# First weights in quarters on SyncE's queue, x1 to x3 on ScalarE's, and the first splits in a written order

## The chip, the cores and the metric

One core of a Trainium2 chip runs the whole program. The metric is device microseconds (us) of one launch. TensorE multiplies, ScalarE and VectorE prepare its operands, GpSimd does a few small jobs, and SyncE and ScalarE issue the DMA transfers that bring inputs from the chip's memory into the on-chip memory.

## The reference, cut to what matters

The reference is a two-layer decoder trunk on 256 tokens of width 1024. Each layer is: half of a gated feed-forward block, a mixing part, and another half block. Only the very first block matters here:

```
h = h + 0.5 * swiglu(rms_norm(h, g), w_gate, w_up, w_down)      # DM = 1024, DFF = 2816
rms_norm(x, g) = x * rsqrt(mean(x*x) + 1e-6) * g
swiglu(x, wg, wu, wd) = (silu(x @ wg) * (x @ wu)) @ wd
```

Everything else (convolution, two kinds of attention, shared keys and values, the other three half blocks) is the same before and after.

## The kernel before, in words

**Layout.** The input is held transposed: `x` is 128 partitions by 8 tiles ("x0" to "x7") by 256 tokens, so tile k holds features 128k to 128k+127. All weights lie in one array of chunks, each 128 partitions by 2048 columns (1 MB), in the order of use; a chunk is used in two halves of 1024 columns, a half is eight 128x128 weight tiles.

**Precision.** Every product is made of two-part operands. A weight tile is split into a high part `wh` (ScalarE copy to a shorter format, function `hi`, L215) and a low part `wl` (VectorE subtraction of `wh` from the raw weight, `lo`, L219). The activations are split the same way: `scaled_split` (L289) writes `y` high, x times the gain (ScalarE L295, or VectorE L293 for even tiles here), and then `y` low (VectorE L296). For one weight tile, one product of 512 columns takes `wh` with both parts of `y` side by side, and one of 256 columns takes `wl` with the high part.

**The opening.** The normalisation factor is applied after the products, so the products can start before all of x is there. The first two gate tiles and the first two up tiles are summed at once, with the features k in the outer loop: for each k four `wh` products and four `wl` products (L386 to L396, output tiles `ag` and `au`). Chunk 0 and chunk 1 are packed for that: 512 columns, a "quarter" of a chunk, hold the four weight tiles of one k. Chunk 0 serves k = 0 to 3, chunk 1 serves k = 4 to 7. From chunk 2 on (the third gate tile, j = 2) a half is one output tile over all eight k.

**Queues before.** ScalarE issues the gains `vt` (L142). SyncE issues, in this order, x0, quarter 0 of chunk 0, x1, quarter 1, x2 and x3 together, the second half of chunk 0 in one transfer, x4 to x7 (L147 and L149), and then chunk 1 and chunk 2 in halves (L197 and L198), later chunks whole (L200).

**Engine orders.** A planner that simulates the program sets each engine's order of instructions, except where the code writes an order: `A`, `V`, `G` and `mmul` chain an engine's instructions when its letter is in `state["order"]`. Before, only TensorE ("P") is chained in the opening. The eight splits of x stand ahead of the block (L721 and L722), the eight squares for the mean (L403) and their sum (L407) behind it; where these land between the weight splits on ScalarE and VectorE is the planner's choice.

**Products that nobody reads.** Ten products on a constant tile run at the start (L137, output `pw`), while no data is there. Eight more (`KEEP`, L392 and L393) stand between the `wh` and `wl` products of k = 1.

**After the opening.** The sum of squares `aacc` feeds a tiny product (`anrp`), whose result is broadcast (`anbp`) and used from j = 3 on.

Of the kernel before, what the change touches and what calls it, by code (L numbers as in the profile page):

```python
# [9 lines left out]
F32 = mybir.dt.float32  # L10
# [7 lines left out]
P = 128  # L18
DM = 1024
KD = DM // P  # L20
SEQ = 256
# [16 lines left out]
CH = 2048  # L38
HC = 1024
NB = 2 * MW  # L40
WARM = 10
KEEP = {(1, 0): 8}
MASKED = 1e30

MEM_AT = 9
# [70 lines left out]
def tile_kernel(ctx: ExitStack, tc: tile.TileContext, w, xT, memT, pos, vec, hg, const, wave, bias, taps, out):  # L116
# [22 lines left out]
    nc.vector.memset(onec, 1.0 / DM)  # L139

    warm = cp.tile([P, 1], F32, name="warm")
    nc.scalar.dma_start(vt[:, :V_LG], vec[:, :V_LG])  # L142
    raw0 = wp.tile([P, CH], F32, name="raw0", tag="raw", bufs=3)
    q = HC // 2
    for tiles, cols in ((slice(0, 1), slice(0, q)), (slice(1, 2), slice(q, HC)), (slice(2, 4), slice(HC, CH)),
                        (slice(4, KD), None)):
        nc.sync.dma_start(x[:, tiles], xT[:, tiles])  # L147
        if cols is not None:
            nc.sync.dma_start(raw0[:, cols], w[0][:, cols])  # L149
    nc.scalar.activation(warm, onec, AF.Silu)  # L150
    mhalf = cp.tile([P, 16], F32, name="mhalf")
    nc.vector.memset(mhalf, -0.5)
# [188 lines left out]
    def ffn(name, y, acc, nexts, store=False, hook=None, after=None, hook_down=None, r=None, plan=None):  # L341


        state["low_at"] = LOW_AT
        plan = plan or {}
        rows_at = [j for (j, _, _), what in plan.items() if what == "rows"]
        n = KF * 2 * SEQ
        hs = cp.tile([P, n + P], F32R, name=name + "hs", tag="hs")
        hs = hs[:, GATED_AT:GATED_AT + n].rearrange("p (k h s) -> p k h s", k=KF, h=2)
        first = acc is None  # L350
        rb = None if r is None else bcast_rows(name + "nb", r)
        halves = {}
        norm = {"r": r}

        def mean():
            norm["r"] = rstd_cols(name + "nr", acc)

        def rows():
            norm["rb"] = bcast_rows(name + "nb", norm["r"])

        def planned(j, which):
            return {k: {"mean": mean, "rows": rows}.get(what, what) for (jj, w_, k), what in plan.items()
                    if (jj, w_) == (j, which)}

        def gated(j, g, h, rb):
            nc.vector.tensor_tensor(g, g, rb, op=ALU.mult)
            s = tp.tile([P, SEQ], F32, name=f"{name}s{j}", tag="s")
            state["func"] = nc.scalar.activation(s, g, AF.Silu)
            if store:
                nc.gpsimd.tensor_tensor(s, s, rb, op=ALU.mult)  # L370
            if callable(h):
                h = h()
            nc.vector.tensor_tensor(h, h, s, op=ALU.mult)
            nc.scalar.activation(hs[:, j, 0], h, AF.Copy)
            nc.vector.tensor_tensor(hs[:, j, 1], h, hs[:, j, 0].bitcast(F32), op=ALU.subtract)

        for j in range(KF):
            if hook and j > 1:
                with tc.issue_after(state["act"].ins), tc.issue_after(state["dve"].ins), \
                        tc.issue_after(state["sync"].ins):  # L380
                    hook(j)
            if first and j == 0:

                four = [psum(f"{name}{'gu'[i % 2]}{i // 2}") for i in range(4)]
                it = tiles_of(4)
                state["order"] = "P"  # L386
                for k in range(KD):
                    wts = [next(it) for _ in four]
                    for o, (wh, _) in zip(four, wts):
                        mmul(o, wh, y[:, k].rearrange("p a s -> p (a s)"), start=k == 0, stop=False)  # L390
                    for at in range(2):
                        for i in range(KEEP.get((k, at), 0)):  # L392
                            mmul(pw, busy[:, :P], busy, start=True, stop=True)  # L393
                        if at == 0:
                            for o, (_, wl) in zip(four, wts):
                                mmul(o[:, :SEQ], wl, y[:, k, 0], start=False, stop=k == KD - 1)  # L396
                state["order"] = ""
                acc = new_acc(name + "acc0")
                behind(nc.scalar.dma_start(cst, const), state["act"])

                sq = cp.tile([P, KD, SEQ], F32, name="sq0", tag="kv")
                for k in range(KD):
                    nc.scalar.activation(sq[:, k], x[:, k], AF.Square)  # L403
                n = KD
                while n > 1:
                    n //= 2
                    add = nc.vector.tensor_tensor(acc if n == 1 else sq[:, :n].rearrange("p k s -> p (k s)"),  # L407
                                                  sq[:, :n].rearrange("p k s -> p (k s)"),
                                                  sq[:, n:2 * n].rearrange("p k s -> p (k s)"), op=ALU.add)
                    if n == KD // 2:  # L410
                        behind(add, state["dve"])
            if first and j < 2:
                pg, pu = four[2 * j:2 * j + 2]
            else:

                at = ("sc", 2) if first and j == 2 else ()
                pg, pu = psum(f"{name}g{j}", *at), psum(f"{name}u{j}", *at)
                if j == 0:

                    wts = [list(tiles_of(1)) for _ in range(2)]  # L420
                    for ks in (range(KD - 1), (KD - 1,)):
                        for o, wt in zip((pg, pu), wts):
                            for k in ks:
                                mm2(o, wt[k], y, k, k == 0, k == KD - 1)
                else:
                    mm_group2(pg, y, planned(j, "g"))
                    mm_group2(pu, y, planned(j, "u"))
            if j == 0 and "mean" not in plan.values() and r is None:
                mean()
            if rb is None and j < rows_at[0]:  # L430
                halves[j] = pg, pu
                if j < 2:
                    halves[j] = both_halves(f"{name}gs{j}", pg, "g"), both_halves(f"{name}h{j}", pu, "h")
                continue
            if rb is None:
                rb = norm["rb"]
            halves[j] = pg, pu
            for i in sorted(halves):
                g, h = halves.pop(i)
                if i > 1 or not rows_at:  # L440
                    g, h = both_halves(f"{name}gs{i}", g, "g"), (lambda i=i, h=h: both_halves(f"{name}h{i}", h, "h"))
                gated(i, g, h, rb)
        if after:
            tables(after)
        ys = [y_tiles(f"{name}y{i}", Y_AT.get(f"{name}y{i}", 16)) for i in range(len(nexts))]
        acc = new_acc(name + "acc")
        it = tiles_of(KD * KF // 8)
        for m in range(KD):
            po = psum(f"{name}o{m}")
            if hook_down:  # L450
                with tc.issue_after(state["act"].ins):
                    hook_down(m)

            both_sums = m < KD - 1
            for k in range(KF):
                if both_sums:
                    mm2(po, next(it), hs, k, k == 0, k == KF - 1)
                else:
                    mm3(po[:, :SEQ], next(it), hs, k, k == 0, k == KF - 1)
            if store:  # L460
                d = both_halves(f"{name}d{m}", po, "g") if both_sums else po[:, :SEQ]
                nc.vector.scalar_tensor_tensor(x[:, m], d, 0.5, x[:, m], op0=ALU.mult, op1=ALU.add)
                nc.sync.dma_start(out[m], x[:, m])
                continue
            if both_sums:
                d = both_halves(f"{name}d{m}", po, "g")
                nc.vector.scalar_tensor_tensor(d, d, 0.5, rb, op0=ALU.mult, op1=ALU.mult)
            else:
                d = tp.tile([P, SEQ], F32, name=f"{name}d{m}", tag="g")
                nc.vector.scalar_tensor_tensor(d, po[:, :SEQ], 0.5, rb, op0=ALU.mult, op1=ALU.mult)  # L470
            nc.vector.tensor_tensor(x[:, m], d, x[:, m], op=ALU.add)
            for yy, g in zip(ys, nexts):
                state["ends"] = scaled_split(yy, x[:, m], m, g)
            square_sum(f"{name}q{m}", acc, x[:, m], m == 0)
        state["low_at"] = 0
        return ys, acc
# [241 lines left out]


    y = y_tiles("y0")  # L720
    for k in range(KD):  # L721
        scaled_split(y, x[:, k], k, V_FFN1, k % 2 == 0)  # L722
    kv0 = []

    def prepare(j):
# [797 lines left out]
```

## Time and profile before

| | |
|---|---|
| median of 3 runs | 945.51 us (945.45 to 945.63) |
| profiled execution, its own time | 946.09 us |
| its span on the core | 944.3 us |
| TensorE busy | 937.6 us, 99% of the span |
| VectorE busy | 716.4 us, 76% |
| ScalarE busy | 563.2 us, 60% |
| granted TensorE clock in the page's slices | 9 tenths or more in all 40 |

The span runs from the first to the last instruction of the program in one profiled execution; what that execution's own time has beyond it (946.09 - 944.3 = 1.8 us) lies outside the program's instructions. Rows of the timeline give the start, the duration, the engine, the source line, the tiles written and read, and in square brackets how long the engine had been idle and what ended the idle time. SPq and ACTq are SyncE's and ScalarE's sequencers issuing DMA transfers.

### The profile page before, as it was taken

To read this page: it belongs to the slowest core of one execution; us is meant where nothing else is said; L and a number is where in the kernel's file an instruction comes from. 1 tells how busy PE (TensorE), PEld (TensorE's weight loads), DVE (VectorE), ACT (ScalarE), POOL (GpSimd) and SP (SyncE) were. 2 spreads that over 40 slices of the span, in tenths; PEclk is the share of its full clock that TensorE was granted. 3 is DMA by queue.
4 is the path that set the end of the run, shared out by engine and by line. 5 is a ranking of instruction groups with operands and counts; after the bars stand their busy time and mean duration, and the time that the engine had idled before them with its cause. 6 is when DMAs were issued, how large, how long until landed. Compare 5 with 4: busy or idle time off the path is not lost.

```text
span 944.3 us, 15093 instructions
## 1 busy us (share of the span) xinstructions
PE 937.6 (99%) x5696; PEld 822.6 (87%) x5696; DVE 716.4 (76%) x1235; ACT 563.2 (60%) x1026; POOL 129.9 (14%) x123
## 2 busy tenths in 40 slices
PE   9999999999999999999999999999999999999998
PEld 6888888888789888888988888888997998888887
DVE  7898877767897877767767777777779578777653
ACT  6776666554576655655546655655548666565542
POOL 0122000112223000000123000000134133222100
PEclk9999999999999999999999999999999999999999
DMA  8855455554334655555555555555551345555560
GB/s 299 294 190 206 179 191 209 180 186 171 129 127 159 219 212 182 188 211 180 188 191 196 185 181 204 195 184 203 193 179 62 117 177 183 200 200 180 208 217 20
DMA packets 26936, 174.16 MB, mean 184 GB/s; under 512 B 3376, under 2 KB 5136, under 8 KB 6512
## 3 DMA queue, kind: packets, MB, share of 16 engines
q1 hardware_dynamic: 26576, 173.04, 52.2%
q8 instruction: 44, 0.72, 0.3%
q14 instruction: 28, 0.23, 0.1%
q10 hardware_dynamic: 288, 0.17, 0.1%
HBM read 172.15 MB, written 1.05 MB: 183 GB/s over the span
## 4 chain that ended last, share of the span: by engine, by line
PE 95%; DVE 3%; DMA 1%; ACT 1%; SPq 0%; issue 0%; ACTq 0%
PE do L184 6%; PE co L184 6%; PE bo L184 6%; PE ao L184 6%; PE bg L184 6%; PE cg L184 6%; PE dg L184 6%; PE cu L184 6%; PE bu L184 6%; PE du L184 6%; PE ag L184 6%; PE au L184 6%; PE kv L184 3%; PE obo L184 2%; PE oao L184 2%; PE M L184 1%
## 5 line engine op out<-in xcount | busy, mean ns | idle before, releaser
L215 ACT ACTIVATE wh<-raw 128x1024 fp32r<-128x1024 f32 (+1 forms) x326 | 341.7, 1050 | 322.9 <-PE do L184 25.1
L219 DVE TENSOR_TENSOR wl<-raw,wh 128x1024 fp32r<-128x1024 f32 (+1 forms) x326 | 397.0, 1219 | 163.9 <-ACT wh L215 162.8
L184 PE MATMUL ag<-y,wh 128*128 128x512 f32 x176 | 62.5, 393 | 0.7 <-ACT wh L215 0.7
L184 PE MATMUL au<-y,wh 128*128 128x512 f32 x176 | 62.2, 391 | 0.0
L184 PE MATMUL bg<-oay,wh 128*128 128x512 f32 x176 | 61.4, 390 | 0.0
L184 PE MATMUL dg<-oby,wh 128*128 128x512 f32 x176 | 61.4, 390 | 0.0
L184 PE MATMUL cg<-by,wh 128*128 128x512 f32 x176 | 61.3, 390 | 0.0
L184 PE MATMUL bu<-oay,wh 128*128 128x512 f32 x176 | 61.3, 389 | 0.0
L184 PE MATMUL du<-oby,wh 128*128 128x512 f32 x176 | 61.2, 389 | 0.0
L184 PE MATMUL cu<-by,wh 128*128 128x512 f32 x176 | 61.2, 390 | 0.0
L184 PE MATMUL ao<-ahs,wh 128*128 128x512 f32 (+1 forms) x198 | 60.1, 365 | 0.0
L184 PE MATMUL bo<-bhs,wh 128*128 128x512 f32 (+1 forms) x198 | 60.1, 365 | 0.0
L184 PE MATMUL co<-chs,wh 128*128 128x512 f32 (+1 forms) x198 | 60.1, 365 | 0.0
L184 PE MATMUL do<-dhs,wh 128*128 128x512 f32 (+1 forms) x198 | 60.1, 365 | 0.0
L184 PE MATMUL cg<-by,wl 128*128 128x256 f32 x176 | 48.8, 277 | 0.0
L184 PE MATMUL ag<-y,wl 128*128 128x256 f32 x176 | 48.7, 279 | 0.0
L184 PE MATMUL bg<-oay,wl 128*128 128x256 f32 x176 | 48.7, 277 | 0.0
L184 PE MATMUL dg<-oby,wl 128*128 128x256 f32 x176 | 48.7, 277 | 0.0
L184 PE MATMUL cu<-by,wl 128*128 128x256 f32 x176 | 48.6, 276 | 0.0
L184 PE MATMUL bu<-oay,wl 128*128 128x256 f32 x176 | 48.6, 276 | 0.0
L184 PE MATMUL du<-oby,wl 128*128 128x256 f32 x176 | 48.6, 276 | 0.0
L184 PE MATMUL ao<-ahs,wl 128*128 128x256 f32 x176 | 48.6, 277 | 0.0
(948 smaller groups left out, 2330.4 us busy)
## 6 DMA issues: line engine op xcount, KB each, us to landing
raw<-in_w SPq DMA_DIRECT2D x158, 1024.0 KB, 4.8
raw<-in_w SPq DMA_DIRECT2D x5, 512.0 KB, 9.5
mT<-in_memT SPq DMA_DIRECT2D x1, 1024.0 KB, 9.7
out<-x SPq DMA_DIRECT2D x8, 128.0 KB, 1.7
raw<-in_w SPq DMA_DIRECT2D x2, 256.0 KB, 4.0
x<-in_xT SPq DMA_DIRECT2D x1, 512.0 KB, 8.1
spec<-in_bias SPq DMA_DIRECT2D x1, 384.0 KB, 8.9
tapw<-in_taps SPq DMA_DIRECT2D x1, 288.0 KB, 10.0
```

Of the source, the lines that this page charges most:

```text
L184: return in_order("P", nc.tensor.matmul(*a, **k))
L215: state["act"] = nc.scalar.activation(wh[:, s], raw[:, s], AF.Copy)
L219: state["dve"] = nc.vector.tensor_tensor(wl[:, s], raw[:, s], wh[:, s].bitcast(F32), op=ALU.subtract)
```

## The change

- ScalarE now issues `vt`, x1, and x2 with x3. SyncE issues x0, the four quarters of chunk 0 one by one, x4 to x7, and then chunk 1 as before.
- The opening gets a written order on TensorE, ScalarE and VectorE ("PAV"). For each k: the high part of y (VectorE for k = 0, ScalarE for all others), the low part of y, `hi` and `lo` of that k's quarter, then the eight products. The squares of x0, x1 and x2 stand at k = 0, 2 and 3, those of x3 and x4 behind k = 7, then the first half of chunk 2 is split, then come the squares of x5 to x7.
- The eight unread products at k = 1 are gone, and the unread products at the start are nine instead of ten.

```diff
-WARM = 10
-KEEP = {(1, 0): 8}
+WARM = 9
...
-    nc.scalar.dma_start(vt[:, :V_LG], vec[:, :V_LG])
...
-    for tiles, cols in ((slice(0, 1), slice(0, q)), (slice(1, 2), slice(q, HC)), (slice(2, 4), slice(HC, CH)),
-                        (slice(4, KD), None)):
-        nc.sync.dma_start(x[:, tiles], xT[:, tiles])
-        if cols is not None:
-            nc.sync.dma_start(raw0[:, cols], w[0][:, cols])
+    nc.scalar.dma_start(vt[:, :V_LG], vec[:, :V_LG])
+    for tiles in (slice(1, 2), slice(2, 4)):
+        nc.scalar.dma_start(x[:, tiles], xT[:, tiles])
+    nc.sync.dma_start(x[:, :1], xT[:, :1])
+    for c in range(0, CH, q):
+        nc.sync.dma_start(raw0[:, c:c + q], w[0][:, c:c + q])
+    nc.sync.dma_start(x[:, 4:], xT[:, 4:])
...
-                it = tiles_of(4)
-                state["order"] = "P"
+                acc = new_acc(name + "acc0")
+                sq = cp.tile([P, KD, SEQ], F32, name="sq0", tag="kv")
+
+                def square(k):
+                    A(nc.scalar.activation(sq[:, k], x[:, k], AF.Square))
+
+                state["order"] = "PAV"
                 for k in range(KD):
-                    wts = [next(it) for _ in four]
...
+                    if k % 2 == 0:
+                        wh, wl, parts, hi, lo = half_hi()
+                    gain = vt[:, V_FFN1 + k:V_FFN1 + k + 1]
+                    if k == 0:
+                        square(0)
+                        V(nc.vector.tensor_scalar(y[:, k, 0], x[:, k], gain, None, op0=ALU.mult))
+                    else:
+                        A(nc.scalar.activation(y[:, k, 0], x[:, k], AF.Copy, scale=gain))
+                    V(nc.vector.scalar_tensor_tensor(y[:, k, 1], x[:, k], gain, y[:, k, 0].bitcast(F32), op0=ALU.mult,
+                                                     op1=ALU.subtract))
+                    A(hi(parts[k % 2]))
+                    if k in (2, 3):
+                        square(k - 1)
+                    V(lo(parts[k % 2]))
+                    at = [slice((k % 2 * 4 + i) * P, (k % 2 * 4 + i + 1) * P) for i in range(4)]
+                    for o, c in zip(four, at):
+                        mmul(o, wh[:, c], y[:, k].rearrange("p a s -> p (a s)"), start=k == 0, stop=False)
+                    for o, c in zip(four, at):
+                        mmul(o[:, :SEQ], wl[:, c], y[:, k, 0], start=False, stop=k == KD - 1)
+                behind(nc.scalar.dma_start(cst, const), state["act"])
+                square(3)
+                square(4)
+                wh, wl, parts, hi, lo = half_hi()
+                A(hi(parts[0]))
+                V(lo(parts[0]))
+                state["made"].append((wh, wl))
+                for k in range(5, KD):
+                    square(k)
                 state["order"] = ""
-                acc = new_acc(name + "acc0")
-                behind(nc.scalar.dma_start(cst, const), state["act"])
...
     y = y_tiles("y0")
-    for k in range(KD):
-        scaled_split(y, x[:, k], k, V_FFN1, k % 2 == 0)
```

More of the change, by code (lines that the diff above doesn't have):

```diff
@@ L384, in ffn @@
                 four = [psum(f"{name}{'gu'[i % 2]}{i // 2}") for i in range(4)]
-                it = tiles_of(4)
-                state["order"] = "P"
-                for k in range(KD):
-                    wts = [next(it) for _ in four]
[L389 to L396, printed above, removed]
@@ L397, in ffn @@
-                state["order"] = ""
-                acc = new_acc(name + "acc0")
-                behind(nc.scalar.dma_start(cst, const), state["act"])
-                sq = cp.tile([P, KD, SEQ], F32, name="sq0", tag="kv")
-                for k in range(KD):
-                    nc.scalar.activation(sq[:, k], x[:, k], AF.Square)
+                acc = new_acc(name + "acc0")
+                sq = cp.tile([P, KD, SEQ], F32, name="sq0", tag="kv")
+                def square(k):
+                    A(nc.scalar.activation(sq[:, k], x[:, k], AF.Square))
@@ L720, in tile_kernel @@
     y = y_tiles("y0")
-    for k in range(KD):
-        scaled_split(y, x[:, k], k, V_FFN1, k % 2 == 0)
     kv0 = []
```

## The prediction

> **What bounds the kernel now.** I read the page first, then the busy times by stage, the timeline of the first 20 us, the waits and the chain of waits.
>
> ```profile
> span 944.3 us, 15093 instructions
> PE 937.6 (99%) x5696; PEld 822.6 (87%) x5696; DVE 716.4 (76%) x1235; ACT 563.2 (60%) x1026; POOL 129.9 (14%) x123
> ```
> ```profile
> 5.28:14.35 9.07, 8.35 (x42) 5.95 (x40) 6.25 (x15) 6.43 (x16) 0.00 (x0) 1.00 0.99 368
> 14.35:20.05 5.70, 5.70 (x32) 5.00 (x33) 5.70 (x9) 3.53 (x5) 0.00 (x0) 1.00 0.87 308
> ```
>
> TensorE is the bound for nearly the whole span. The change touches only the opening, so a gain can come only from TensorE's time there, and all of it shifts the rest one to one. From 14.35 us TensorE is busy without a gap: 5.70 us for 32 products, the last four of the eight k, so 1.42 us for one k. Eight k need 8 x 1.42 = 11.4 us. They took from 5.33 to 20.05, 14.7 us: 3.3 us of standing or unread work is all that could be won at that start. The next rows (timeline) say where.
>
> ```profile
> 1.44 4.33 PE L137 MATMUL pw<-busy 128*128 128x512 bf16 x10 [1.44 <-DVE mhalf L152]
> 4.00 0.63 SPq L197 DMA_DIRECT2D raw<-in_w  x1
> 4.65 0.63 ACT L215 ACTIVATE wh<-raw 128x512 fp32r<-128x512 f32 x1 [0.80 <-DMA raw<-in_w]
> 5.33 0.67 PE L184 MATMUL ag<-y,wh 128*128 128x512 f32 x1
> 5.57 0.51 ACT L295 ACTIVATE y<-x,vt 128x256 fp32r<-128x256 f32 x1 [0.30 <-DMA x<-in_xT]
> 6.76 0.63 ACT L215 ACTIVATE wh<-raw 128x512 fp32r<-128x512 f32 x1 [0.37 <-DMA raw<-in_w]
> 8.24 0.40 PE L184 MATMUL au<-y,wh 128*128 128x512 f32 x1
> 8.48 1.90 PE L184 MATMUL pw<-busy 128*128 128x512 bf16 x8
> 8.95 0.35 DVE L293 TENSOR_SCALAR y<-x,vt 128x256 fp32r<-128x256 f32 x1 [2.35 <-DMA x<-in_xT]
> 9.22 0.68 DVE L219 TENSOR_TENSOR wl<-raw,wh 128x512 fp32r<-128x512 f32 x1
> 10.03 0.47 PE L184 MATMUL ag<-y,wl 128*128 128x256 f32 x1
> 10.35 1.15 ACT L215 ACTIVATE wh<-raw 128x512 fp32r<-128x512 f32 x2 [0.28 <-DMA raw<-in_w]
> 11.04 0.50 PE L184 MATMUL ag<-y,wh 128*128 128x512 f32 x1 [0.19 <-ACT wh L215]
> 13.69 0.61 ACT L215 ACTIVATE wh<-raw 128x512 fp32r<-128x512 f32 x1
> 14.21 2.61 ACT L215 ACTIVATE wh<-raw 128x512 fp32r<-128x512 f32 x4
> 14.36 0.50 PE L184 MATMUL ag<-y,wh 128*128 128x512 f32 x1 [0.26 <-ACT wh L215]
> 20.05 0.39 PE L184 MATMUL ag<-y,wh 128*128 128x512 f32 x1
> ```
> ```profile
> 3.52 8.09 DMA x<-in_xT
> 11.64 0.91 ACT y L295 x2
> 12.55 1.23 ACT sq L403 x4
> 13.78 0.53 ACT wh L215
> 14.36 0.50 PE ag L184
> ```
> ```profile
> raw<-in_w SPq DMA_DIRECT2D x1, 512.0 KB, 8.9
> ```
>
> Arrivals read from these rows: quarter 0 at 4.65, x1 at 5.57, quarter 1 at 6.76, x2 and x3 at 8.95, the second half of chunk 0 at 10.35, x4 to x7 at 3.52 + 8.09 = 11.61. The last row is the landing of the first half of chunk 1, whose issue is the row at 4.00: 4.00 + 8.9 = 12.90. Two waits are of the kernel's own making. At k = 1 VectorE sits 2.35 us on the split of x2 with quarter 1's `lo` queued behind it (8.95, 9.22), and the eight unread products fill that hole. Before k = 4 the chain shows four squares, 1.23 us, ahead of `hi`, so TensorE starts k = 4 at 14.36 though its weights were there at 12.90. The rest of the 3.3 us is waiting for data.
>
> **The change part by part.** The end of the opening is set by the last k that has to wait, since all later ones run back to back. Before, that is k = 4 (14.36). After, k = 4 again: it needs x4 to x7 and the first half of chunk 1, and the bytes ahead of that half are the same.
>
> ```profile
> L215 ACT ACTIVATE wh<-raw 128x512 fp32r<-128x512 f32 x5 | 2.8, 615 | 0.0
> L403 ACT ACTIVATE sq<-x 128x256 f32<-128x256 f32 x4 | 1.3, 402 | 0.0
> L219 DVE TENSOR_TENSOR wl<-raw,wh 128x512 fp32r<-128x512 f32 x6 | 3.8, 688 | 0.3 <-ACT wh L215 0.3
> L219 DVE TENSOR_TENSOR wl<-raw,wh 128x1024 fp32r<-128x1024 f32 x4 | 4.8, 1221 | 0.0
> L296 DVE SCALAR_TENSOR_TENSOR y<-x,vt,y 128x256 fp32r<-128x256 f32 x4 | 1.7, 480 | 0.0
> L407 DVE TENSOR_TENSOR sq<-sq 128x512 f32<-128x512 f32 x1 | 0.7, 686 | 0.0
> ```
>
> - *Written order, k = 4.* No squares stand ahead of its `hi`, and its y is split while the weights are on their way (11.61 + 0.51 + 0.48, under 12.90). Start: 12.90 + 0.61 + 0.05 (4.65 + 0.63 to 5.33 is the same step) = 13.56, against 14.36: a gain of **0.80 us**, if the half of chunk 1 lands as before.
> - *Written order, k = 1.* VectorE no longer waits for x2, so `lo` of k = 1 comes 0.68 us behind its `hi`, under the four `wh` products. This wins up to 1.8 us there (8.24 + 0.23 to 10.03), all of it lost again while k = 4 waits for data: 0.
> - *Unread products.* The eight filled that hole: 0. The tenth at the start ends 0.43 us earlier now; the real products behind it have slack, below: 0.
> - *Transfers.* x1, x2 and x3 move to ScalarE's queue and pass SyncE's pieces. Between 4.65 and 5.57 x1 took 0.92 us of the one queue; interleaved with quarter 0 it can delay that quarter by nothing to 0.92 us, so k = 0 starts between 5.33 and 6.25. Quarter 1 shares with x2 and x3: somewhere between 6.76 and 8.95, k = 1 between 7.4 and 9.6. The second half of chunk 0 now comes in two pieces; k = 3 must start by 13.56 - 1.42 = 12.1, so quarter 3 may land up to 11.5, 1.1 us later than the whole half did. All this is covered by the wait for chunk 1; without that cover it would cost the 0.92 us.
> - *The landing of chunk 1's half* is the unknown. Later: two quarters instead of one half. Quarter 1 took 6.76 - 5.57 = 1.19 us of the queue, two would take 2.4; the half took 10.35 - 8.95 = 1.40: +1.0 us. Earlier: the rates below. 265 GB/s over 6 us are 1.59 MB, which at 410 take 3.9 us: -2.1 us if a second queue filled what the first leaves. I take 0, between the two: the same bytes on the same 16 DMA engines, which the profile has at shares of 0.83 and 0.94.
>
> ```profile
> 2.00:5.00 3.00, 3.00 (x9) 1.06 (x7) 0.84 (x2) 1.42 (x4) 0.00 (x0) 1.00 0.83 265
> 5.00:8.00 3.00, 2.72 (x13) 1.93 (x11) 1.18 (x2) 1.72 (x4) 0.00 (x0) 1.00 0.94 266
> 8.00:14.30 6.30, 5.91 (x31) 4.02 (x29) 5.03 (x12) 4.93 (x13) 0.00 (x0) 1.00 1.01 410
> ```
>
> - The Trainium skill, page "DMA: Bandwidth & Descriptors", section "Issuing engines are not separate DMA queues", says that transfers issued from several engines run on the same 16 DMA engines and interleave, and that only issue time is saved. By that rule the -2.1 us end would not occur and the sum would stay at 0.80 or less; the row with 0.83 beside 265 GB/s leaves room that the rule does not speak of.
> - *What is late next: chunk 2.* k = 4 starts at 13.56, so j = 2 starts at 13.56 + 5.70 = 19.26 and needs `wl` of chunk 2's first half 0.23 later, 19.49. ScalarE: `hi` of k = 4 ends at 13.51; three more k at 0.46 + 0.52 each (0.91 for two y, the `hi` at 13.69 and 14.21) bring 16.4; two squares 0.62, `hi` of 1024 columns 1.06: 18.1; `lo` 1.22: 19.35. It just fits, by 0.1 us. Cost 0, at most 0.3.
>
> Sum: profiled 946.09 = span 944.3 + 1.8 around it. Span after 944.3 - 0.80 = 943.5, own time 945.3. The median of the runs shown is 0.58 below the profiled time, so **945.51 - 0.80 = 944.7 us**.
>
> **The rivals.**
>
> *B, the pieces are slower.* The half of chunk 1 lands 1.0 us later, k = 4 starts at 14.56, 0.2 later than before: 945.7. For it: early transfers run at 265 GB/s. Against: the rate rises to 410 at 8 us, before the second half of chunk 0 (10.35) and x4 to x7 (11.61) have landed, so part of the slowness belongs to the first 8 us and not to the pieces.
>
> *C, two queues fill the engines.* From a landing 1.1 us earlier on (11.8) the gain passes 1.9 us. At the end of the bound, 10.8, k = 4 could start at 11.5, just behind k = 3 if k = 0 starts by 5.8: gain 2.9. Taken in the middle, 2.4: 943.1. For it the share of 0.83; against it the share of 0.94 at the same rate in the next 3 us.
>
> *D, the clock falls: slower than before.* The unread products ran at 0.43 us each at the start and at 0.24 at k = 1, so TensorE has a half pace, though the clock column shows 1.00 throughout. In the opening of before it never stood longer than this row's last number:
>
> ```profile
> PE ag L184 <- ACT wh L215: 0.7, 3, 0.3
> ```
>
> After, it stands about 1 us before k = 1 and again before k = 4 (k = 3 ends near 12.5). If such a stand brings the half pace back for as long as the start showed it, 4.3 us, then 4.3 us cover 2.15 us of work: 944.7 + 2.15 = 946.9. It decides from the length of the stand, which no row bounds between 0.3 and 1 us; against it, TensorE works well over half of every 3 us. The Trainium skill, page "TensorE: Matmul & The Clock Gate", section "Part 1: The HAM clock gate (the "warmup" mystery)", puts the fall behind an idle window of about 3.4 us. By that rule stands of 1 us cost nothing.
>
> *E, the wait moves to the mean.*
>
> ```profile
> 20.76 0.42 DVE L407 TENSOR_TENSOR aacc<-sq 128x256 f32<-128x256 f32 x1
> 23.82 0.50 PE L184 MATMUL anrp<-onec,aacc 128*128 128x1 f32 x4
> ```
>
> The sum of squares now comes behind chunk 2's `lo` (19.35) and the squares of x5 to x7. VectorE then needs 1.22 (1024 columns, as a `lo` of that size) + 0.69 + 0.42 for the sum and 1.22 for each half of a chunk let in between: `aacc` at 22.9 or 24.1. TensorE asked for it 3.77 us into j = 2, after the change at 23.0. It could stand 1.1 us with all later products queued behind it: 945.8. Against: this product isn't chained, so the planner can move it on.
>
> **How the numbers follow.** Forecast 0.52, B 0.14, C 0.16, D 0.08, E 0.10. About 0.2% (1.9 us) is what a measurement of this kernel can tell from no change. Only C is beyond it on the fast side: 0.16. D alone is 1.4 us slower than before; together with B or E it passes 1.9 us: 0.04. The rest is 0.80. The likeliest one's own range is 944.1 to 945.5. For 8 in 10 I reach to C's end on one side and to D on the other: 942.7 to 946.8.
>
> **What would show it.** k = 4's first `wh` product starts near 13.6 and j = 2 near 19.3, with no gap between. The `hi` of k = 4 stands straight behind the landing of chunk 1's first half, with no square ahead. `lo` of k = 1 follows its `hi` at once. Wrong would be: that landing far from 12.9 (B, C), real products 0.46 us apart after a stand (D), TensorE idle before `anrp` or at j = 2 (E and the chunk 2 step). A shift of the rest of the kernel other than k = 4's would say that the planner's order changed further on.

## The result

The changed kernel takes **952.14 us** (median; 951.76 to 952.40) against 945.57 for the kernel before in the same comparison: a ratio of 1.0067, 95% interval 1.0054 to 1.0079. It is 6.6 us slower, outside the predicted range of 942.7 to 946.8 and on the other side. The profiled execution took 951.91 us.

The page of the changed kernel, its first lines and the group that has grown most (busy time, mean of one, idle time before it and what ended it):

```profile
span 950.0 us, 15087 instructions
PE 938.6 (99%) x5687; PEld 824.2 (87%) x5687; DVE 716.1 (75%) x1232; ACT 564.4 (59%) x1029; POOL 129.6 (14%) x123
...
L184 PE MATMUL ag<-y,wh 128*128 128x512 f32 x176 | 64.7, 404 | 5.4 <-DVE ags L270 4.5
```

The span grew by 5.7 us (944.3 to 950.0); the profiled execution of the kernel before lies 0.5 us above its median and that of the changed kernel 0.2 us below, so this is less than the 6.6 us of the medians. The gate tiles of the first block have 5.4 us of idle time before them, 4.5 of it ended by VectorE's `ags` (L270), the step that adds the two halves of a finished gate tile out of the product memory. Before, no product of the block waited for that step. The timeline of the changed kernel, TensorE and the few steps of the other engines that matter:

```profile
1.44 4.02 PE L136 MATMUL pw<-busy 128*128 128x512 bf16 x9 [1.44 <-DVE mhalf L152]
6.31 0.79 PE L184 MATMUL ag<-y,wh 128*128 128x512 f32 x1 [0.85 <-ACT wh L215]
7.14 0.63 ACT L215 ACTIVATE wh<-raw 128x512 fp32r<-128x512 f32 x1 [0.48 <-DMA raw<-in_w]
7.80 0.69 DVE L219 TENSOR_TENSOR wl<-raw,wh 128x512 fp32r<-128x512 f32 x1 [0.42 <-ACT wh L215]
9.03 0.63 PE L184 MATMUL ag<-y,wh 128*128 128x512 f32 x1
11.75 0.63 ACT L215 ACTIVATE wh<-raw 128x512 fp32r<-128x512 f32 x1 [0.64 <-DMA raw<-in_w]
13.91 0.40 PE L184 MATMUL ag<-y,wh 128*128 128x512 f32 x1
16.74 1.23 DVE L219 TENSOR_TENSOR wl<-raw,wh 128x1024 fp32r<-128x1024 f32 x1 [0.64 <-ACT wh L215]
19.46 0.39 PE L184 MATMUL ag<-y,wh 128*128 128x512 f32 x1
24.03 0.41 DVE L425 TENSOR_TENSOR aacc<-sq 128x256 f32<-128x256 f32 x1
29.11 0.50 PE L184 MATMUL anrp<-onec,aacc 128*128 128x1 f32 x4
33.77 0.38 PE L187 MATMUL anbp<-cst,anr 128*128 128x128 f32 x2
36.38 0.28 PE L184 MATMUL au<-y,wl 128*128 128x256 f32 x1
40.60 0.42 DVE L270 TENSOR_TENSOR ags<-ag,ags3c 128x256 f32<-128x256 f32 x1
41.16 0.69 PE L184 MATMUL ag<-y,wh 128*128 128x512 f32 x1 [4.51 <-DVE ags L270]
41.65 0.41 PE L184 MATMUL ag<-y,wl 128*128 128x256 f32 x1
41.87 0.63 PE L184 MATMUL ag<-y,wh 128*128 128x512 f32 x1
45.58 0.39 PE L184 MATMUL au<-y,wh 128*128 128x512 f32 x1
```

Read downwards: k = 0 starts at 6.31, k = 1 at 9.03, k = 4 at 13.91, and the block's third gate tile (j = 2) at 19.46, 0.59 us earlier than before (20.05). So the opening did gain. The mean's product `anrp` then runs at 29.11 (before 23.82) although its input `aacc` is there at 24.03 + 0.41. The broadcast `anbp` runs at 33.77. For the kernel before, the two steps that answer to this:

```profile
28.66 0.38 PE L187 MATMUL anbp<-cst,anr 128*128 128x128 f32 x2
...
34.98 0.42 DVE L270 TENSOR_TENSOR ags<-ag,ags3c 128x256 f32<-128x256 f32 x1
```

TensorE then stands 4.51 us until 41.16, and behind that it runs at half pace. The busy times of that stage in the changed kernel:

```profile
41.10:44.90 3.80, 3.74 (x13) 3.23 (x14) 3.70 (x12) 2.50 (x7) 0.00 (x0) 0.55 0.63 252
```

The columns are the length, the busy time of PE, PEld, DVE, ACT and POOL with their counts, the clock, the share of the DMA engines and GB/s. Thirteen products and a clock of 0.55; the rows at 41.16, 41.65 and 41.87 show a pair in 0.7 us instead of 0.34. The gate tile of j = 5 takes 45.58 - 41.16 = 4.42 us instead of 16 x 0.17 = 2.72. The sum: -0.59 (opening) + 4.51 (standing) + 1.70 (half pace) = +5.6 us, against 5.7 in the span.

**Why TensorE stands.** The chain of waits of the changed kernel around that place (start, length, what):

```profile
33.93 0.22 PE anbp L187 x2
34.15 1.38 PE ag L184 x8
...
35.56 1.07 ACT wh L215
...
38.55 1.13 DVE wl L219
39.68 0.34 DVE ah L373
40.01 0.33 DVE ags L366
...
40.68 0.34 DVE ags L270
...
41.16 4.58 PE ag L184 x16
```

The products of four tiles find room in the product memory (`psum`, four buffers of the tag "mm"). The gate and up tiles of j = 3 and j = 4 fill them. The gate tile of j = 3 can be emptied only when it is finished, and in VectorE's order its evacuation (adding its two halves out of that memory) stands behind the gating of j = 0 and 1, which needs the broadcast, and behind splits of later weights (`wl` in the chain). The gate tile of j = 5 waits for that buffer. In the code, the broadcast sits inside the gate tile of j = 3 (behind the `wh` product of k = 3), and the rest of that tile is chained behind it. So everything hangs on how much of TensorE's other work is put ahead of the broadcast. Counted in TensorE's order from j = 2 on: before, 47 products ahead and 49 between the broadcast and j = 5; in the changed kernel 81 ahead and only 15 behind. The planner pulled the rest of the up tile of j = 3 (8 products), the whole gate tile of j = 4 (16) and ten products of its up tile forward. From the broadcast to the end of the evacuation it takes 35.40 - 28.66 = 6.7 us before and 41.02 - 33.77 = 7.2 after. Forty-nine products cover that (8.3 us); fifteen (2.6 us) leave 4.6 us of standing.

### The profile page after: what moved, and what is told of

Its sections match the earlier page's. It is cut to its first block, busy times and chain, and to the rows that moved or that the text cites. A ratio compares the mean times of both kernels' runs of the same rounds, so it can differ in the third digit from the quotient of the medians.

```text
span 950.0 us, 15087 instructions
## 1 busy us (share of the span) xinstructions
PE 938.6 (99%) x5687; PEld 824.2 (87%) x5687; DVE 716.1 (75%) x1232; ACT 564.4 (59%) x1029; POOL 129.6 (14%) x123
## 4 chain that ended last, share of the span: by engine, by line
PE 95%; DVE 3%; ACT 1%; DMA 0%; issue 0%; POOL 0%; SPq 0%; ACTq 0%
PE ag L184 7%; PE do L184 6%; PE co L184 6%; PE ao L184 6%; PE bo L184 6%; PE dg L184 6%; PE au L184 6%; PE bg L184 6%; PE cg L184 6%; PE cu L184 6%; PE du L184 6%; PE bu L184 6%; PE kv L184 3%; PE obo L184 2%; PE oao L184 2%; PE M L184 1%
## 5 line engine op out<-in xcount | busy, mean ns | idle before, releaser
L184 PE MATMUL ag<-y,wh 128*128 128x512 f32 x176 | 64.7, 404 | 5.4 <-DVE ags L270 4.5
L184 PE MATMUL au<-y,wl 128*128 128x256 f32 x176 | 48.8, 279 | 0.0
```

The lines of the kernel that those rows point to most:

```text
L184: return in_order("P", nc.tensor.matmul(*a, **k))
```

## The experiments

Theory T1 is the one just told. Rivals: the moved transfers delay later chunks (T2), the sum of squares comes too late whatever TensorE's order (T3).

**Transfers alone.** The kernel before with this and nothing else:

```diff
-    for tiles, cols in (...):          # x0, quarter 0, x1, quarter 1, x2-3, second half, x4-7 on SyncE
+    for tiles in (slice(1, 2), slice(2, 4)):
+        nc.scalar.dma_start(x[:, tiles], xT[:, tiles])
+    nc.sync.dma_start(x[:, :1], xT[:, :1])
+    for c in range(0, CH, q):
+        nc.sync.dma_start(raw0[:, c:c + q], w[0][:, c:c + q])
+    nc.sync.dma_start(x[:, 4:], xT[:, 4:])
```

> The kernel before with the transfers of the change alone (x1 to x3 on ScalarE's queue, chunk 0 in quarters); the orders of all engines and the unread products stay as before. Theory T1 (the loss comes from where TensorE's order puts the two products of the mean, which the written order of the opening moved): TensorE's order is that of before, so no standing at 36 us; the time is 945.6 or up to 1 us less, since chunk 1's first half lands earlier (11.7 instead of 12.9) but four squares still stand ahead of its split. Rival T2 (the loss comes from the transfers, which delay later chunks): slower by 4 us or more, with a standing before j = 5.

945.73 against 945.74 us, ratio 0.9999 (0.9990 to 1.0008): no change. The broadcast runs at 27.87 and nothing stands. The profiled span is 943.5, and j = 2 starts at 19.26; the runs don't confirm that as a gain. T2 falls.

**Order alone.** The changed kernel with that same hunk undone.

> The changed kernel with the transfers of before: the written order and the fewer unread products alone. T1: the two products of the mean stand where they do in the changed kernel, so TensorE stands 4 to 5 us before j = 5 and runs at half pace for about 3 us behind it: 951.5 to 953. T2: 945 to 946.

953.19 us, ratio 1.0072 (1.0058 to 1.0086). Its waits of TensorE, and a stage of its opening:

```profile
PE ag L183 <- DVE ags L269: 4.5, 1, 4.5
PE ag L183 <- ACT wh L214: 2.4, 2, 1.8
```
```profile
11.20:15.70 4.50, 4.50 (x17) 3.89 (x18) 4.26 (x8) 4.47 (x11) 0.00 (x0) 0.62 1.00 377
```

The same 4.5 us before j = 5: the written order brings it, the transfers don't. The second row is new: in the opening TensorE stood 1.8 us for k = 2, and from 12 to 15.5 us ran at half pace (clock 0.62 in that stage). In the kernel before, the eight unread products filled such a stand.

**TensorE in program order.** The changed kernel, with this:

```diff
                 for k in range(5, KD):
                     square(k)
-                state["order"] = ""
+                state["order"] = "P"          # "" again at j == 5
...
-    plan={(2, "u", 1): "mean", (3, "g", 3): "rows"}
+    plan={(2, "u", 7): "mean", (3, "g", 7): "rows"}
```

> The changed kernel, with TensorE chained in program order up to j = 4, the mean's product at the up tile j = 2, k = 7 and the broadcast at the gate tile j = 3, k = 7: 47 products of the block stand ahead of the broadcast from j = 2 on, as in the kernel before, against 81 in the changed kernel. T1: the broadcast runs near 27.5 us, the gate tile of j = 3 is evacuated 7 us later, long before j = 5 asks for its buffer; no standing, no half pace at 41 us: the opening's 0.6 us are left, 944.6 to 945.3. Rival T3 (the sum of squares itself comes too late, 24.4 against 21.2 us, wherever its product stands): TensorE waits 1 to 3 us at the mean's product or at the broadcast instead, 946 to 948.

945.31 us, ratio 0.9996 (0.9987 to 1.0005): the whole loss is gone, and the opening's 0.5 us (j = 2 at 19.59) can't be told from no change. Its timeline:

```profile
24.91 0.50 PE L184 MATMUL anrp<-onec,aacc 128*128 128x1 f32 x4
28.11 0.38 PE L187 MATMUL anbp<-cst,anr 128*128 128x128 f32 x2
```

The sum is as late as in the changed kernel (23.78 + 0.41), yet nothing waits for it. T3 falls: the place of the products did the harm, not the time of the sum.

**Late squares in the kernel before.**

```diff
-                    nc.scalar.activation(sq[:, k], x[:, k], AF.Square)
+                    behind(nc.scalar.activation(sq[:, k], x[:, k], AF.Square), state["act"])
```

> The kernel before with the eight squares behind the last split of chunk 1 on ScalarE, nothing else changed; the planner then puts 62 products ahead of the broadcast instead of 47 and leaves 34 between it and j = 5 instead of 49. T1: 34 products of 0.17 us are 5.8 us, the evacuation of the gate tile j = 3 takes 6.7 to 7.2 us from the broadcast on, so TensorE stands 0.9 to 1.4 us before j = 5; k = 4 starts 0.8 us earlier since no squares stand ahead of its split; in all 0 to 0.7 us slower, 945.6 to 946.3, the standing to be seen in the waits. If the late squares as such did the harm, whatever TensorE's order: 949 or more.

946.47 us, ratio 1.0010 (1.0001 to 1.0019), just above what was expected. Late squares alone, a step like one of the written order's, make the planner move the broadcast behind 62 products instead of 47. TensorE stands 0.57 us before the up tile of j = 5; 0.9 to 1.4 us before its gate tile were expected. From the broadcast (30.62) to the end of the evacuation (36.53) it took 5.9 us here, less than the 6.7 to 7.2 of the count.

**The broadcast alone, in the kernel before.** The opening stays as it was:

```diff
-                    plan={(2, "u", 1): "mean", (3, "g", 3): "rows"})
+                    plan={(2, "u", 1): "mean", (4, "u", 3): "rows"})     # the other kernel: (4, "g", 3)
```

> The kernel before, with its own transfers, orders and unread products; only the broadcast of the mean is emitted at the up tile j = 4, k = 3 instead of the gate tile j = 3, k = 3. The mean's product stays where it was. 9 products (1.5 us) are left between the broadcast and j = 5, against 49 before and 15 in the changed kernel. T1 (TensorE stands before j = 5 for 6.7 to 7.2 us less the products left, and then runs at half pace for some 3 us): a standing of 5.2 to 5.7 us, 952 to 954. If the place of the broadcast alone does no harm without the late sum: 945.6 to 947.

952.68 us, ratio 1.0072 (1.0057 to 1.0087).

> The same with the broadcast at the gate tile j = 4, k = 3: 25 products (4.3 us) are left. T1: a standing of 2.4 to 2.9 us before j = 5; with half pace behind it for up to 3.4 us 949 to 950.5, without 948 to 948.6. Otherwise 945.6 to 946.5.

950.41 us, ratio 1.0049 (1.0032 to 1.0066). Rows of the two timelines, the first kernel in the first fence:

```profile
35.32 0.38 PE L187 MATMUL anbp<-cst,anr 128*128 128x128 f32 x2
41.38 0.47 PE L184 MATMUL ag<-y,wh 128*128 128x512 f32 x1 [4.20 <-DVE ags L270]
```
```profile
32.30 0.38 PE L187 MATMUL anbp<-cst,anr 128*128 128x128 f32 x2
39.55 0.76 PE L184 MATMUL ag<-y,wh 128*128 128x512 f32 x1 [2.67 <-DVE ags L270]
40.33 0.63 PE L184 MATMUL ag<-y,wh 128*128 128x512 f32 x1
```

The kernel before, with its own opening and its early sum, gets the loss of the changed kernel from that one key. This is the most direct of the tests: the place of the broadcast in TensorE's order is enough. One thing moves with the key: in the code, the gating of j = 0 to 3 is now emitted behind j = 4. In the first of the two kernels VectorE ran the same steps from the broadcast to the evacuation, in the same order, as in the changed kernel. With nine products left I expected 5.2 to 5.7 us of standing and saw 4.2: from the broadcast to the end of the evacuation (40.81 + 0.42) it took 5.9 us there, not 6.7 to 7.2. The sign and the place come out of the count; the size only to within about 1.5 us. The second row of the second kernel is at half pace: 2.67 us of standing are enough for it.

**Squares beside their own k, in the changed kernel.** The sum may start right behind k = 7.

```diff
-                    if k in (2, 3):
-                        square(k - 1)
+                    if k:
+                        square(k)
...
-                square(3)
-                square(4)
-                wh, wl, parts, hi, lo = half_hi()
-                A(hi(parts[0]))
-                V(lo(parts[0]))
-                state["made"].append((wh, wl))
-                for k in range(5, KD):
-                    square(k)
```

> The changed kernel with every square beside its own k and the sum of squares free to start behind k = 7; chunk 2's first split isn't part of the written order. The planner leaves 32 products (5.4 us) between the broadcast and j = 5 instead of 15. T1: a standing of 1.3 to 1.8 us instead of 4.5, no half pace behind it: 947 to 948.2. If the standing doesn't go by the products left: 951 to 952.5.

947.36 us, ratio 1.0017 (1.0008 to 1.0027).

```profile
36.91 0.50 PE L184 MATMUL ag<-y,wh 128*128 128x512 f32 x1 [1.25 <-DVE ags L270]
37.25 0.28 PE L184 MATMUL ag<-y,wl 128*128 128x256 f32 x1
...
40.85 0.50 PE L184 MATMUL au<-y,wh 128*128 128x512 f32 x1 [0.87 <-DVE ah L270]
```

32 products left, 1.25 us of standing where 1.3 to 1.8 were expected, another 0.87 us before the up tile that wasn't expected, and full pace behind the first (a pair in 0.35 us from 37.36 on).

| kernel | products between broadcast and j = 5 | longest standing before a tile of j = 5 | half pace behind it |
|---|---|---|---|
| before | 49 | 0 | |
| program order | 49 | 0 | |
| late squares | 34 | 0.57 us | no |
| squares beside | 32 | 1.25 us | no |
| broadcast at (4, "g", 3) | 25 | 2.67 us | yes |
| changed kernel, and order alone | 15 | 4.51 us | yes |
| broadcast at (4, "u", 3) | 9 | 4.20 us | yes |

**The half pace by itself.** The changed kernel with 21 unread products (`fill`) put between the last product of j = 4 and the first of j = 5.

```diff
+                if first and j == 5:
+                    fill = psum("fill", "aux", 2)
+                    state["order"] = "P"          # "" again behind the gate tile
+                    for i in range(21):
+                        mmul(fill, busy[:, :P], busy, start=True, stop=True)
```

> The changed kernel with 21 unread products, 4.5 us at full pace, where TensorE stands before j = 5. If the half pace behind it (41.2 to 44.4 us) comes from the standing alone: the first products of j = 5 run at 0.34 us a pair, 1.5 to 1.9 us less than the changed kernel, 950.2 to 950.6. If it comes from something else at that place, a transfer or the evacuation: 951.8 to 952.4.

950.47 us, ratio 1.0049 (1.0037 to 1.0062), 1.7 us less than the changed kernel.

```profile
36.47 4.71 PE L184 MATMUL fill<-busy 128*128 128x512 bf16 x21
41.13 0.47 PE L184 MATMUL ag<-y,wh 128*128 128x512 f32 x1
41.44 0.28 PE L184 MATMUL ag<-y,wl 128*128 128x256 f32 x1
```

J = 5 starts at the same moment and runs at full pace. So the half pace behind the standing comes from the standing, and costs the 1.4 to 1.7 us that the sum gave it (the spans differ by 950.0 - 948.6 = 1.4).

**Thirteen unread products at the start**, in the changed kernel:

```diff
-WARM = 9
+WARM = 13
```

> The changed kernel with 13 unread products at the start instead of 9, nothing else. Theory C1 (the half pace of the first two k, 6.31 to 10.3 us, comes from TensorE standing 0.85 us between the ninth unread product and the first real one): TensorE stays busy until 6.3, the first real products run at full pace, 1.4 us for k = 0, and j = 2 starts at 17.8 to 18.2 instead of 19.5. Of that 1.4 to 1.7 us the whole may reach the end (950.4) or little (952), since the broadcast's evacuation stands behind chunk 5's split on VectorE. Rival C2 (the pace rises at a moment of its own, whatever stands ahead): k = 0 still takes 2.7 us, j = 2 at 19.5, 952.

951.28 us, ratio 1.0060 (1.0048 to 1.0073), between the two expectations.

```profile
6.45 0.51 PE L184 MATMUL ag<-y,wh 128*128 128x512 f32 x1
...
7.97 0.40 PE L184 MATMUL ag<-y,wh 128*128 128x512 f32 x1
17.80 0.39 PE L184 MATMUL ag<-y,wh 128*128 128x512 f32 x1
```

k = 0 takes 1.5 us instead of 2.7, and j = 2 starts at 17.80 instead of 19.46. The half pace of the first two k in the profiled execution of the changed kernel cost 1.66 us of the opening, and C1's forecast holds there: with no stand ahead, full pace. At the end of the kernel 1.4 us of it arrive in the two profiled spans (950.0 to 948.6), but this profiled execution is the fastest of its five. The medians differ by 0.9 us (952.14 to 951.28) and the intervals of the two ratios overlap, so a gain over all executions isn't shown. C1 isn't the whole story either. In the kernel with the squares beside, nine unread products and a longer stand ahead of k = 0 were followed by full pace, 0.33 us to the next product:

```profile
1.44 3.58 PE L136 MATMUL pw<-busy 128*128 128x512 bf16 x9 [1.44 <-DVE mhalf L152]
6.35 0.50 PE L184 MATMUL ag<-y,wh 128*128 128x512 f32 x1 [1.33 <-ACT wh L215]
6.68 0.39 PE L184 MATMUL au<-y,wh 128*128 128x512 f32 x1
```

The first row tells the two cases apart: here the nine unread products took 3.58 us, in the changed kernel 4.02. The pace had risen before the stand began. In the changed kernel, program order and the filled stand, the nine took 4.02 us, all at half pace, a stand of 0.85 to 0.89 us followed, and the pace rose only near 10.3 to 10.8 us. And with no stand at all, late squares ran the first three products of k = 0 at half pace, to near 7.0 us. So a stand went with a late rise where the pace had not yet risen; each of these is a single execution.

**Program order and thirteen.** As the third experiment, but:

```diff
-WARM = 9
+WARM = 13
...
-    plan={(2, "u", 7): "mean", (3, "g", 7): "rows"}
+    plan={(3, "g", 3): "mean", (3, "u", 3): "rows"}
```

> The changed kernel with TensorE in program order up to j = 4, the mean's product at the gate tile j = 3, k = 3, the broadcast at the up tile j = 3, k = 3, and 13 unread products at the start. T1 and C1: no standing before j = 5 and no half pace, j = 2 starts near 18: 943.5 to 944.2. If the later place of the broadcast already costs a standing at j = 5: up to 1 us more.

**944.20 us, ratio 0.9985 (0.9976 to 0.9994): faster than both kernels**, by 1.4 us (0.15%) against before.

```profile
6.31 0.50 PE L184 MATMUL ag<-y,wh 128*128 128x512 f32 x1
...
18.47 0.39 PE L184 MATMUL ag<-y,wh 128*128 128x512 f32 x1
```

J = 2 starts at 18.47, 1.58 us earlier than before, and TensorE stands nowhere behind it up to 60 us; the span is 942.6, 1.7 less than before. With 41 products left there is no standing at j = 5.

**A written sum.** On the third experiment, with 13 unread products and the squares beside their k:

```diff
+                half()                 # hi and lo of the next half chunk, chained on ScalarE and VectorE
+                add(4)                 # one step of the sum of squares, chained on VectorE
+                half()
+                add(2)
+                add(1)
+                half()
```

> The changed kernel with every square beside its own k, the sum of squares and the splits of chunk 2 and of chunk 3's first half in a written order, TensorE in program order up to j = 4 with the mean at j = 2, up, k = 7 and the broadcast at j = 3, gate, k = 7, and 13 unread products at the start. T1 and C1: the sum is there by 22.5 us, the broadcast near 26, no standing anywhere behind the opening, j = 2 at 18: 943.4 to 944.0. If the squares delay the splits of k = 4 to 7: 0.3 to 0.6 us more.

945.50 us, ratio 0.9997 (0.9988 to 1.0005): a miss. J = 2 started at 18.24, 1.8 us earlier than before, but from there to j = 5 it took 18.80 us instead of 17.11. The sum was there at 23.26 and its product ran at 24.14, but VectorE's next step for it (`anrv`, at 26.59) stood behind three splits of 1024 columns. The first of them is the written order's own (the third `half()`), the other two the planner had put ahead. So the broadcast waited:

```profile
28.48 0.43 PE L187 MATMUL anbp<-cst,anr 128*128 128x128 f32 x2 [0.99 <-POOL anr L320]
```

The same lesson once more: writing the order of one part leaves the planner to put other work ahead of what isn't written. The stand of 0.99 us is the larger part of the 1.7 us lost there; the rest wasn't followed.

## Why the prediction was wrong

- **The step that failed is in rival E**: "this product isn't chained, so the planner can move it on". I counted that as a protection. TensorE indeed never waited at the mean's product. The planner moved it from 23.8 to 29.1 us and pulled j = 4 ahead of the broadcast, and the wait came back at j = 5 as a lack of product buffers, 4.5 us long instead of at most 1.1. The prediction named the two products and their times, but never asked who waits for the broadcast and how many products stand between it and the next tile that needs a buffer.
- **With it failed the frame**: "a gain can come only from TensorE's time there, and all of it shifts the rest one to one". A written order in the opening changes what the planner does with everything that isn't written, 20 us further on. It was named as the last thing that could go wrong, without a price or a chance.
- **Rival D** was right that half pace can come back behind a stand, and misplaced. The changed kernel ran at half pace behind the 4.51 us of standing (1.7 us, where 2.15 was priced), and had no stand before k = 4. Order alone shows it in the opening, as rival D had it, from k = 2 on, behind stands of 0.56 and 1.79 us. The page "TensorE: Matmul & The Clock Gate" of the Trainium skill, section "Part 1: The HAM clock gate (the "warmup" mystery)", was cited for stands of 1 us costing nothing. Stands of 0.57 and 1.25 us agree with that; but 1.79 and 2.67 us, well below its idle window of about 3.4 us, were followed by half pace. The measurements decide: its figure isn't a safe bound here.
- **"The tenth at the start: 0", "all this is covered by the wait for chunk 1"**: wrong. Nine products end at 5.46, k = 0 starts at 6.31 (0.06 past the predicted 5.33 to 6.25), and k = 0 and k = 1 ran at half pace until 10.3. The cover was gone, because the half of chunk 1 was there at 11.75 and not at 12.90. So k = 4 was held by products, not by data. That is a second term mis-sized: 1.66 us of the opening in the profiled execution instead of 0.
- **"k = 4 near 13.6, j = 2 near 19.3"**: 13.91 and 19.46, near, but by luck. The earlier landing (-1.15 us, within the bounds of +1.0 and -2.1) and the half pace nearly cancelled.
- **The landing.** Rates in the changed kernel:

```profile
2.00:5.00 3.00, 3.00 (x9) 0.91 (x6) 0.83 (x2) 1.90 (x3) 0.00 (x0) 1.00 0.85 220
5.00:8.00 3.00, 2.15 (x6) 1.40 (x5) 1.29 (x3) 1.89 (x4) 0.00 (x0) 1.00 0.94 332
8.00:14.30 6.30, 6.30 (x31) 5.49 (x31) 5.12 (x10) 5.28 (x13) 0.00 (x0) 1.00 1.03 420
```

  By 8 us 3 x (220 + 332) = 1656 KB had come, against 3 x (265 + 266) = 1593 before: 4% more, 0.15 us of the 1.15 at 420 GB/s. The Trainium skill, page "DMA: Bandwidth & Descriptors", section "Issuing engines are not separate DMA queues", says that transfers issued from several engines run on the same 16 DMA engines; the nearly equal rates agree with that. What failed is the premise "the bytes ahead of that half are the same". When the half landed, about 1656 + 3.75 x 420 = 3231 KB had come in the changed kernel (11.75) and 1593 + 4.90 x 410 = 3602 before (12.90). So 371 KB less of later transfers came ahead of it, 0.9 us at 420 GB/s. SyncE issued the half behind it at 5.62 us instead of 4.68; whether that is the reason wasn't tested.
- **Right:** `lo` of k = 1 follows its `hi` at once (7.80 behind 7.14 + 0.63); no squares stand ahead of k = 4's `hi`; chunk 2's `lo` is in time (17.97 for 19.46).

What stays open: which line of the written order moved the broadcast from 47 to 81 products. Late squares account for 62 in the kernel before; putting the squares beside their k and taking chunk 2 out of the written order brings the changed kernel back to 64 only. The rest lies in the planner's own simulation, which no profile shows.

## What to carry to other kernels

Where a planner orders what isn't written, writing one part of the order is a change to all of it: look, beyond the lines edited, at the next small step with a long tail behind it (here a broadcast that lets buffers go), count the work that stands between it and the first instruction that needs its buffers, and compare that with the length of the tail. If the count must hold, write it: TensorE chained in program order up to j = 4 took the whole loss away. And when unread products are taken out, follow the first real product: in the profiled execution a stand of under a microsecond at the start went with 1.7 us of lost pace, of which the medians show 0.9 us, not clear of noise.

## What the hardware showed unexpectedly

TensorE's half pace came back behind stands of 1.79 us (with another of 0.56 us that ended 1.7 us earlier), 2.67, 4.20 and 4.51 us, and not behind 0.57, 1.25 or, in the opening of the kernel with the squares beside, 1.33 us. It did not always begin with the next product: in order alone the first products behind the stand (11.20) still ran at full pace and the half pace began near 12.0. It lasted 3.3 us in the changed kernel (41.16 to 44.43) and about 2.9 us behind the stand of 2.67 us. The moment at which the pace first rises isn't fixed either: near 5.5 us in the kernel before, near 7.0 in late squares and near 10.3 in the changed one, with the first product at 1.44 us in all three. The clock column shows the half pace behind a stand (0.55, 0.62), but 1.00 during the unread products of the start, which run at 0.43 us each, and 1.00 again from 5.46 to 10.30 us in the changed kernel; there only the spacing of the products tells.
